# An encoder block on one core: norm rows queued behind weight splits, and TensorE kept in program order in the mixed part

## Chip, core and metric

The kernel runs on one core of one Trainium2 chip. TensorE (PE; its weight loads are PEld) multiplies into eight PSUM banks, VectorE (DVE) and ScalarE (ACT) work beside it on SBUF and PSUM, GpSimd (POOL) does a few small operations, and SyncE (SP) issues the DMAs. The metric is device time in microseconds, the median of the runs of one kernel. A line number such as L868 is a line of the kernel's file; the lines of the changed kernel stand up to eleven further down than those of the kernel before, and its new statements have numbers of their own.

## What is computed

One layer of an encoder, in float32, for 256 tokens of width 2048:

```python
mix = hybrid_mixer(x, ...)                     # grouped-query attention and latent attention
x = layer_norm(ALPHA * x + mix, ln1_g, ln1_b)
mem_n = layer_norm(mem, mem_ln_g, mem_ln_b)
xa = memory_cross_attention(x, mem_n, ...)     # 4 heads, 256 memory tokens
x = layer_norm(ALPHA * x + xa, ln2_g, ln2_b)
ff = squared_relu_mlp(x, w_mlp_in, w_mlp_out)  # jnp.square(relu(h @ w_in)) @ w_out, 8192 hidden
x = layer_norm(ALPHA * x + ff, ln3_g, ln3_b)
```

The change lies in the second layer norm's last step and in the MLP.

## The kernel before

**Products of split numbers.** Every float32 operand of a product is split into a high part (written by ACT, L87 or L936) and a low part (source minus high part, written by DVE, L88 or L937). `mm3` (L162 to L165) multiplies high by high, high by low and low by high into one PSUM bank. A 1 MB weight block `raw` arrives by one DMA and is split in pieces of 128x1024. High parts rotate through four buffers `w_hi`, low parts in the MLP through four fixed buffers `lo0` to `lo3`: a piece can be split only when the matmuls of the fourth piece before it are done.

**From cross attention to the MLP.** The matmuls L715 end the cross attention; `add_cross` adds them to `res`, `bn_stats` (L517) and two small operations give mean and deviation, L733 scales, TensorE transposes (L745), and `convert` (L750, L752, L762 or L87, L88) makes `x2t`, the MLP's transposed and split input. Ten matmuls on ones (L785) stand in a pause. All this is in program order. The residual copy `res` also needs gain and bias of the norm: `residual("ln2")` puts 16 row operations of 128x512 (L572) on the list `side`, whose entries are called one by one (`pump`) between weight splits. Those are not bound to an order, so the scheduler that builds the program places them by its own timing, and may move them ahead.

**The MLP.** The hidden layer has 4 chunks of 16 tiles of 128 columns. The first 8 tiles are computed as two groups of four (`hidden_group`, L212 and L217): group 0 with `first_pair` between its pairs of k-tiles, group 1 after it. All other tiles are mixed with the second matrix in `one_pass`, eight passes (chunk c, half q). Its list `items` alternates a hidden tile "g" (L979 and L987, 16 matmuls of 128x512 and 16 of 128x256) with a unit "u", which multiplies a pair of hidden tiles by a 1 MB block of the second matrix. Six units of each pass but the last go by a seven-product scheme (a "seven", 21 matmuls), which needs sums of the weights (`s_t`, L924) and of the hidden pair (L883); the other two take 24 matmuls. The seven products use the banks x11, x12, x21, x22 (acc) and p1, p5, p6, p7 (att). A hidden tile borrows x22, p6, p1 or p7.

**Emptying a hidden tile.** `evacuate` copies one half by ACT (L867), adds the other by DVE (L868); `finish` does relu and square (L872, L873), splits into `ht`, makes the sums and splits them into `aux`. The copy, the result and the sums are tiles `tmp`, from a ring of three.

**What sets the order.** `queue` chains the MLP's splits and weight sums on ACT and on DVE in program order, each engine by itself. The matmuls of the mixed part are not chained: the scheduler interleaves them. SP issues its DMAs in a fixed order, each when its buffer is free.

Of the kernel before, what the change touches and what calls it, by code (L numbers as in the profile page):

```python
# [38 lines left out]
def encoder_kernel(ctx: ExitStack, tc: tile.TileContext, t, out):  # L39
# [122 lines left out]
    def mm3(ps, ah, al, bh, bl, start, stop):  # L162
        nc.tensor.matmul(ps, ah, bh, start=start, stop=False)  # L163
        nc.tensor.matmul(ps, ah, bl, start=False, stop=False)  # L164
        nc.tensor.matmul(ps, al, bh, start=False, stop=stop)  # L165
# [395 lines left out]
    def residual(name):  # L561
# [284 lines left out]
    raw_x = [late.tile([P, 2048], F32, name=f"raw_x{i}") for i in range(2)]  # L846
    rings["rows"] = ctx.enter_context(tc.tile_pool(name="rows", bufs=2))
# [17 lines left out]
    def evacuate(ps, l, h, i):  # L865
        o = slice(i * S, (i + 1) * S)
        nc.scalar.activation(l[:, o], ps[:, S:2 * S], AF.Copy)  # L867
        nc.vector.tensor_tensor(out=h[:, o], in0=ps[:, 0:S], in1=l[:, o], op=ALU.add)  # L868

    def finish(h, c, p):  # L870
# [6 lines left out]
        if p in SEVEN:  # L877
            a11, a21, a12, a22 = [h[:, o:o + P] for o in range(0, 4 * P, P)]
            s = tmp_tile()
            s1, s2, s3, s4 = [s[:, o:o + P] for o in range(0, 4 * P, P)]  # L880
            for o, a, b, op in ((s1, a21, a22, ALU.subtract), (s3, a11, a21, ALU.subtract),
                                (s2, s1, a11, ALU.subtract), (s4, a12, s2, ALU.add)):
                nc.vector.tensor_tensor(out=o, in0=a, in1=b, op=op)  # L883
# [4 lines left out]
    raws, raw_of, fetched, sums = raw_x, {}, [0], deque()  # L888
    items = []
    for c, q in PASSES:  # L890
# [3 lines left out]
        for u in us:  # L894
            n = 2 if q == 0 and u[3] == CH // 2 - 2 else 1
# [3 lines left out]
    def fetch():  # L899
# [6 lines left out]
        if 1 < n < 5:  # L906
            raws.append(raw_tile())
# [21 lines left out]

    def part(src, hi=None, lo=None):  # L930
# [5 lines left out]
        queue(nc.scalar.activation(hi[:, :w], src, AF.Copy))  # L936
        queue(nc.vector.tensor_tensor(out=lo[:, :w], in0=src, in1=f(hi[:, :w]), op=ALU.subtract))  # L937
# [12 lines left out]
    def hidden_group(nexts, tiles, c, j0, beside=None):  # L950
# [20 lines left out]
    def hidden_tile(it, ps):

        _, c, j = it
        for h_ in range(2):
# [3 lines left out]
            def w_hi(k):  # L978
                nc.tensor.matmul(ps, hi[:, k * P:(k + 1) * P], x2t[:, k0 + k, :],  # L979
                                 start=k0 + k == 0, stop=k0 + k == KT - 1)  # L980
# [5 lines left out]
            for k in range(8):  # L986
                nc.tensor.matmul(ps[:, 0:S], lo[:, k * P:(k + 1) * P], x2t[:, k0 + k, 0:S],  # L987
                                 start=False, stop=False)
# [30 lines left out]
    def one_pass(c, q):  # L1019
# [28 lines left out]
        def more(ps):  # L1048
            nc.vector.tensor_tensor(out=m_t, in0=m_t, in1=ps, op=ALU.add)

        spare, n_seven, n_unit, parts = [], 0, 0, []
        while n_unit < len(order):
            it = step()
            if it[0] == "g":
                if n_unit == 0:
                    ps = x22 if it[1:] == (0, LEAD) else p6
# [10 lines left out]
            if p in sevens:  # L1067
# [218 lines left out]
```

## Time and profile before

| | us |
|---|---|
| median of 3 runs (lowest, highest) | 1121.24 (1120.96, 1121.92) |
| the profiled execution | 1121.22 |
| its span, first to last instruction | 1119.4 |
| PE busy in the span | 1084.9 |
| DVE busy | 938.6 |
| ACT busy | 637.7 |
| mean granted TensorE clock | 0.988 |

The span is 1.8 us shorter than the execution. A row of a timeline gives start, duration, engine, line, operation, output<-input, shapes, and in brackets how long the engine sat idle before it and what ended that. Matmuls overlap, so their durations are longer than the distance from one start to the next. In a row of windows, PEclk 0.50 means that TensorE was granted half its clock.

### The profile page before, as it was taken

To read this page: it belongs to the slowest core of one execution; us is meant where nothing else is said; L and a number is where in the kernel's file an instruction comes from. 1 tells how busy PE (TensorE), PEld (TensorE's weight loads), DVE (VectorE), ACT (ScalarE), POOL (GpSimd) and SP (SyncE) were. 2 spreads that over 40 slices of the span, in tenths; PEclk is the share of its full clock that TensorE was granted. 3 is DMA by queue.
4 is the path that set the end of the run, shared out by engine and by line. 5 is a ranking of instruction groups with operands and counts; after the bars stand their busy time and mean duration, and the time that the engine had idled before them with its cause. 6 is when DMAs were issued, how large, how long until landed. Compare 5 with 4: busy or idle time off the path is not lost.

```text
span 1119.4 us, 15382 instructions
## 1 busy us (share of the span) xinstructions
PE 1084.9 (97%) x5864; PEld 935.1 (84%) x5864; DVE 938.6 (84%) x1331; ACT 637.7 (57%) x925; POOL 38.2 (3%) x45
## 2 busy tenths in 40 slices
PE   8999999999999978899999999999999999999896
PEld 6988899888998867788888888888888888888685
DVE  5878677687788768879899999899999899999676
ACT  6555565546576325657467567566566566566440
POOL 1402000000100000000000000000000000000000
PEclk9999999999999989999999999999999999999898
DMA  9664454466467445445555645556646556546632
GB/s 322 239 225 151 151 188 150 152 235 241 167 223 263 151 132 177 180 143 200 206 186 206 226 166 210 196 185 221 210 169 223 189 188 225 194 182 224 227 113 76
DMA packets 37945, 215.87 MB, mean 193 GB/s; under 512 B 4336, under 2 KB 5232, under 8 KB 14192
## 3 DMA queue, kind: packets, MB, share of 16 engines
q1 hardware_dynamic: 37872, 214.89, 54.1%
q8 instruction: 46, 0.75, 0.3%
q14 instruction: 27, 0.22, 0.1%
HBM read 212.78 MB, written 2.10 MB: 192 GB/s over the span
## 4 chain that ended last, share of the span: by engine, by line
PE 94%; DVE 3%; DMA 2%; issue 1%; ACT 1%; SPq 0%; POOL 0%; DVEq 0%
PE acc L163 13%; PE acc L164 13%; PE acc L165 13%; PE acc L979 12%; PE acc L987 6%; PE att L979 6%; PE att L164 4%; PE att L163 4%; PE att L165 4%; PE att L987 3%; PE acc L205 2%; PE acc L203 2%; PE acc L204 2%; PE att L212 1%; DMA row<-in_ln_g 1%; PE acc L715 1%
## 5 line engine op out<-in xcount | busy, mean ns | idle before, releaser
L87 ACT ACTIVATE w_hi<-raw 128x1024 fp32r<-128x1024 f32 (+2 forms) x142 | 139.8, 992 | 118.2 <-PE acc L165 70.6
L88 DVE TENSOR_TENSOR w_lo<-raw,w_hi 128x1024 fp32r<-128x1024 f32 (+2 forms) x130 | 146.2, 1133 | 59.6 <-ACT w_hi L87 58.5
L937 DVE TENSOR_TENSOR lo<-raw,w_hi 128x1024 fp32r<-128x1024 f32 (+1 forms) x138 | 152.0, 1123 | 14.5 <-issue 4.9
L936 ACT ACTIVATE w_hi<-raw 128x1024 fp32r<-128x1024 f32 (+1 forms) x138 | 130.4, 975 | 34.5 <-PE acc L165 23.1
L979 PE MATMUL acc<-x2t,w_hi 128*128 128x512 f32 x576 | 149.8, 392 | 0.0
L979 PEld LDWEIGHTS acc<-x2t,w_hi 128*128 128x128 f32 x576 | 106.3, 189 | 19.3
L937 DVE TENSOR_TENSOR lo<-s_t,w_hi 128x1024 fp32r<-128x1024 f32 x84 | 102.7, 1222 | 17.5 <-ACT w_hi L936 11.9
L937 DVE TENSOR_TENSOR lo<-raw_x,w_hi 128x1024 fp32r<-128x1024 f32 x94 | 103.8, 1124 | 11.1 <-issue 4.9
L936 ACT ACTIVATE w_hi<-s_t 128x1024 fp32r<-128x1024 f32 x84 | 88.5, 1055 | 27.7 <-PE acc L165 12.0
L936 ACT ACTIVATE w_hi<-raw_x 128x1024 fp32r<-128x1024 f32 x94 | 89.2, 975 | 20.5 <-PE acc L165 10.8
L987 PEld LDWEIGHTS acc<-x2t,lo 128*128 128x128 f32 x576 | 78.6, 190 | 5.6
L979 PE MATMUL att<-x2t,w_hi 128*128 128x512 f32 x320 | 83.3, 392 | 0.0
L164 PE MATMUL acc<-lo,ht 128*128 128x512 f32 x213 | 82.2, 395 | 0.0
L987 PE MATMUL acc<-x2t,lo 128*128 128x256 f32 x576 | 80.3, 282 | 0.0
L867 ACT ACTIVATE tmp<-acc 128x256 f32<-128x256 f32 x40 | 15.2, 384 | 112.6 <-PE acc L979 111.4
L165 PE MATMUL acc<-w_hi,ht 128*128 128x512 f32 x210 | 78.8, 394 | 0.0
L163 PE MATMUL acc<-w_hi,ht 128*128 128x512 f32 x210 | 74.2, 396 | 4.6 <-ACT ht L87 4.6
L164 PE MATMUL acc<-w_lo,xt 128*128 128x512 f32 (+2 forms) x192 | 69.2, 362 | 0.0
L165 PE MATMUL acc<-w_hi,xt 128*128 128x512 f32 (+2 forms) x192 | 69.1, 361 | 0.0
L979 PEld LDWEIGHTS att<-x2t,w_hi 128*128 128x128 f32 x320 | 58.6, 189 | 10.9
L163 PE MATMUL acc<-w_hi,xt 128*128 128x512 f32 (+2 forms) x192 | 65.7, 362 | 1.8 <-ACT w_hi L87 1.8
L165 PE MATMUL acc<-w_hi,ot 128*128 128x512 f32 (+1 forms) x136 | 51.9, 382 | 0.0
(285 smaller groups left out, 2448.0 us busy)
## 6 DMA issues: line engine op xcount, KB each, us to landing
raw<-in_w_mo SPq DMA_DIRECT2D x38, 1024.0 KB, 4.8
raw<-in_w_mc SPq DMA_DIRECT2D x34, 1024.0 KB, 4.8
raw_x<-in_w_mo SPq DMA_DIRECT2D x26, 1024.0 KB, 4.8
raw_x<-in_w_mc SPq DMA_DIRECT2D x22, 1024.0 KB, 4.8
raw<-in_w_out SPq DMA_DIRECT2D x16, 1024.0 KB, 4.9
raw<-in_w_mi SPq DMA_DIRECT2D x8, 1024.0 KB, 4.9
raw<-in_w_b SPq DMA_DIRECT2D x5, 1024.0 KB, 4.8
raw<-in_w_qa SPq DMA_DIRECT2D x16, 256.0 KB, 5.4
```

The source lines that it names most:

```text
L87: pin(nc.scalar.activation(hi, src, AF.Copy), pinned)
L88: return pin(nc.vector.tensor_tensor(out=lo, in0=src, in1=f(hi), op=ALU.subtract), pinned)
L163: nc.tensor.matmul(ps, ah, bh, start=start, stop=False)
L164: nc.tensor.matmul(ps, ah, bl, start=False, stop=False)
L165: nc.tensor.matmul(ps, al, bh, start=False, stop=stop)
L203: nc.tensor.matmul(ps, hi, xt[:, k, 0:S], start=k == 0, stop=False)
L204: nc.tensor.matmul(ps, hi, xt[:, k, S:2 * S], start=False, stop=False)
L205: nc.tensor.matmul(ps, lo, xt[:, k, 0:S], start=False, stop=k == nk - 1)
L936: queue(nc.scalar.activation(hi[:, :w], src, AF.Copy))
L937: queue(nc.vector.tensor_tensor(out=lo[:, :w], in0=src, in1=f(hi[:, :w]), op=ALU.subtract))
L979: nc.tensor.matmul(ps, hi[:, k * P:(k + 1) * P], x2t[:, k0 + k, :], start=k0 + k == 0, stop=k0 + k == KT - 1)
L987: nc.tensor.matmul(ps[:, 0:S], lo[:, k * P:(k + 1) * P], x2t[:, k0 + k, 0:S], start=False, stop=False)
```

## The change

- `residual("ln2")` is replaced: after group 0, gain and bias come whole (two DMAs of 1 MB, into `s_t` and into a new buffer `row_b`), eight row operations of 128x1024 are put on `side` behind four empty entries, and they are chained by `queue`. Group 1's splits are chained too and call two entries each, so the first row operations follow the third split of group 1. A loop in `one_pass` that called what was left on `side` falls away.
- The block buffers `raw_x0`, `raw_x1` become `raw_x` and `row_b`; `row_b` serves from the fifth block on.
- `mm3` and the matmuls of `hidden_tile` go through `queue` in `one_pass`: TensorE runs them in program order.
- In the first pass two hidden tiles lead the first unit instead of one; the second of them borrows bank x21.
- `evacuate` works in place: one `tmp` tile per pair of hidden tiles instead of two. The first two hidden sums become one operation of 128x256, with two signs turned, so p7 is subtracted.

```diff
     def mm3(ps, ah, al, bh, bl, start, stop, keep=lambda ins: ins):
+        keep(nc.tensor.matmul(ps, ah, bh, start=start, stop=False))
+        keep(nc.tensor.matmul(ps, ah, bl, start=False, stop=False))
+        keep(nc.tensor.matmul(ps, al, bh, start=False, stop=stop))
...
-    raw_x = [late.tile([P, 2048], F32, name=f"raw_x{i}") for i in range(2)]
-    rings["rows"] = ctx.enter_context(tc.tile_pool(name="rows", bufs=2))
+    raw_x, row_b = [late.tile([P, 2048], F32, name=w) for w in ("raw_x", "row_b")]
...
-    def evacuate(ps, l, h, i):
+    def evacuate(ps, h, i):
         o = slice(i * S, (i + 1) * S)
-        nc.scalar.activation(l[:, o], ps[:, S:2 * S], AF.Copy)
-        nc.vector.tensor_tensor(out=h[:, o], in0=ps[:, 0:S], in1=l[:, o], op=ALU.add)
+        nc.scalar.activation(h[:, o], ps[:, S:2 * S], AF.Copy)
+        nc.vector.tensor_tensor(out=h[:, o], in0=ps[:, 0:S], in1=h[:, o], op=ALU.add)
...
-            for o, a, b, op in ((s1, a21, a22, ALU.subtract), (s3, a11, a21, ALU.subtract),
-                                (s2, s1, a11, ALU.subtract), (s4, a12, s2, ALU.add)):
-                nc.vector.tensor_tensor(out=o, in0=a, in1=b, op=op)
+            nc.vector.tensor_tensor(out=s[:, 0:2 * P].rearrange("p (i c) -> p i c", c=P),
+                                    in0=a21[:, None, :].broadcast_to([P, 2, P]),
+                                    in1=h.rearrange("p (i c) -> p i c", c=P)[:, 0:4:3, :], op=ALU.subtract)
+            nc.vector.tensor_tensor(out=s2, in0=s1, in1=a11, op=ALU.subtract)
+            nc.vector.tensor_tensor(out=s4, in0=a12, in1=s2, op=ALU.add)
...
-            n = 2 if q == 0 and u[3] == CH // 2 - 2 else 1
+            n = 2 if q == 0 and u[3] == (CH // 2 - 2 if c else 0) else 1
...
-                nc.tensor.matmul(ps, hi[:, k * P:(k + 1) * P], x2t[:, k0 + k, :],
-                                 start=k0 + k == 0, stop=k0 + k == KT - 1)
+                queue(nc.tensor.matmul(ps, hi[:, k * P:(k + 1) * P], x2t[:, k0 + k, :],
+                                       start=k0 + k == 0, stop=k0 + k == KT - 1))
...
-                    ps = x22 if it[1:] == (0, LEAD) else p6
+                    ps = {LEAD: x22, LEAD + 1: x21}[it[2]] if it[1] == 0 else p6
...
-            side.extend(residual("ln2"))
+            for w, row in (("g", s_t), ("b", row_b)):
+                nc.sync.dma_start(row, t[f"ln2_{w}"].partition_broadcast(P))
+                side.extend([lambda o=o, b=b, row=row, op=ALU.mult if w == "g" else ALU.add: queue(
+                    nc.vector.tensor_tensor(out=res[b][:, o:o + 1024], in0=res[b][:, o:o + 1024],
+                                            in1=row[:, o:o + 1024], op=op))
+                    for b in range(NB) for o in (0, 1024)])
+            side.extendleft([lambda: None] * 4)
+            s_in.split, s_in.beside = queued_split, 2
```

Three places of the order follow. **The end of the cross attention.** DVE before: the last addition to `res1` (L699), its statistics (L517, L721, L723), the first scaling (L733); the row operations are those on `row`.

```order
L699 SCALAR_TENSOR_TENSOR res1_1491<-res1_1491,acc_4109 128x256
L572 TENSOR_TENSOR res0_1490<-res0_1490,row_4444 128x512
L517 BN_STATS bn_3937<-res1_1491 128x6
L572 TENSOR_TENSOR res0_1490<-res0_1490,row_4446 128x512
L721 BN_AGGR mv_4146<-bn_3937 128x2
L723 TENSOR_SCALAR rs_v_4148<-mv_4146 128x1
L733 TENSOR_SCALAR res1_1491<-res1_1491,mv_4146,rs_r_4150 128x512
L572 TENSOR_TENSOR res1_1491<-res1_1491,row_4444 128x512
L752 TENSOR_SCALAR tmp_4157<-att_4122,gbt_112 128x256
```

DVE at the same place after the change:

```order
L700 SCALAR_TENSOR_TENSOR res1_1491<-res1_1491,acc_4109 128x256
L518 BN_STATS bn_3937<-res1_1491 128x6
L722 BN_AGGR mv_4146<-bn_3937 128x2
L724 TENSOR_SCALAR rs_v_4148<-mv_4146 128x1
L734 TENSOR_SCALAR res1_1491<-res1_1491,mv_4146,rs_r_4150 128x512
L753 TENSOR_SCALAR tmp_4157<-att_4122,gbt_112 128x256
L763 TENSOR_TENSOR x2t_4038<-tmp_4157,x2t_4038 128x256
```

No row operation stands among the statistics and the first conversions any more. There is none up to the end of group 0; four entries of twice the width follow the third and fourth split of group 1, four the fifth and sixth.

**The first unit of the mixed part.** TensorE after the change: acc_4641 is x21, which the second leading tile has just filled; att_4646 is p7 and att_4645 p6, in banks that the last two tiles of group 1 left.

```order
L984 MATMUL acc_4641<-x2t_4038,w_hi_4710 128x512
L164 MATMUL att_4643<-w_hi_4734,ht_4184 128x512
...
L164 MATMUL att_4646<-w_hi_4749,aux_4185 128x512
...
L164 MATMUL att_4645<-w_hi_4758,aux_4185 128x512
L165 MATMUL att_4645<-lo3_4189,aux_4185 128x512
L166 MATMUL att_4645<-w_hi_4758,aux_4185 128x512
L164 MATMUL acc_4641<-w_hi_4758,ht_4184 128x512
L165 MATMUL acc_4641<-lo3_4189,ht_4184 128x512
L166 MATMUL acc_4641<-w_hi_4758,ht_4184 128x512
L984 MATMUL acc_4642<-x2t_4038,w_hi_4778 128x512 x8
```

DVE after, from the last split of that unit to the operations (L868) that empty the two leading tiles out of acc_4642 and acc_4641:

```order
L934 TENSOR_TENSOR lo3_4189<-s_t_4191,w_hi_4758 128x1024
...
L934 TENSOR_TENSOR lo0_4186<-raw_4607,w_hi_4778 128x1024
L926 TENSOR_TENSOR s_t_4191<-row_b_4193 128x1024
...
L934 TENSOR_TENSOR lo1_4187<-raw_4607,w_hi_4798 128x1024
L868 TENSOR_TENSOR tmp_4624<-att_4432,tmp_4624 128x256
L868 TENSOR_TENSOR tmp_4624<-att_4433,tmp_4624 128x256
L926 TENSOR_TENSOR s_t_4191<-s_t_4191,row_b_4193 128x512 x2
...
L934 TENSOR_TENSOR lo2_4188<-row_b_4193,w_hi_4823 128x1024
L88 TENSOR_TENSOR ht_4184<-tmp_4624,ht_4184 128x2x256
L868 TENSOR_TENSOR tmp_4686<-acc_4642,tmp_4686 128x256
L868 TENSOR_TENSOR tmp_4686<-acc_4641,tmp_4686 128x256
```

DVE before, where the only leading tile is emptied out of x22 (acc_4658): between the two units' splits of block and sums.

```order
L924 TENSOR_TENSOR s_t_4191<-s_t_4191,raw_4619 128x512
L937 TENSOR_TENSOR lo0_4186<-raw_4619,w_hi_4797 128x1024
L937 TENSOR_TENSOR lo1_4187<-raw_4619,w_hi_4811 128x512
L883 TENSOR_TENSOR tmp_4648<-tmp_4639,tmp_4648 128x128
L868 TENSOR_TENSOR tmp_4706<-acc_4658,tmp_4705 128x256
L88 TENSOR_TENSOR aux_4185<-tmp_4648,aux_4185 128x512
L937 TENSOR_TENSOR lo2_4188<-s_t_4191,w_hi_4818 128x1024
L937 TENSOR_TENSOR lo3_4189<-s_t_4191,w_hi_4828 128x1024
```

The first unit's last product writes x21, and the operation that empties x21 stands on DVE behind the splits of the next hidden tile and the first split of the second unit. Before, only x22 was borrowed here, and no product of a seven writes x22.

**The end of the last pass that has hidden tiles.** TensorE before: att_4662 takes the last hidden tile, w_hi_9309 is a part of unit 6, w_hi_9329 of unit 7.

```order
L165 MATMUL acc_4657<-w_hi_9309,ht_4184 128x512
L979 MATMUL att_4662<-x2t_4038,w_hi_9249 128x512 x8
L987 MATMUL att_4662<-x2t_4038,lo2_4188 128x256 x8
L979 MATMUL att_4662<-x2t_4038,w_hi_9270 128x512 x7
L987 MATMUL att_4662<-x2t_4038,lo3_4189 128x256 x8
L979 MATMUL att_4662<-x2t_4038,w_hi_9270 128x512
L163 MATMUL acc_4656<-w_hi_9329,ht_4184 128x512
L164 MATMUL acc_4656<-lo2_4188,ht_4184 128x512
```

TensorE after: att_4646 takes the last hidden tile, w_hi_9213 and w_hi_9228 are parts of unit 6, w_hi_9248 of unit 7.

```order
L984 MATMUL att_4646<-x2t_4038,w_hi_9189 128x512 x7
L992 MATMUL att_4646<-x2t_4038,lo3_4189 128x256 x8
L984 MATMUL att_4646<-x2t_4038,w_hi_9189 128x512
L164 MATMUL acc_4640<-w_hi_9213,ht_4184 128x512
L165 MATMUL acc_4640<-lo0_4186,ht_4184 128x512
...
L166 MATMUL acc_4641<-w_hi_9228,ht_4184 128x512
L164 MATMUL acc_4640<-w_hi_9248,ht_4184 128x512
```

Unit 6 stood ahead of the last hidden tile and now stands between that tile and unit 7.

More of the change, by code (lines that the diff above doesn't have):

```diff
@@ L137, in __init__ @@
             self.ap, self.n, self.fine, self.beside, self.pinned = ap, 0, fine, beside, False
+            self.split = split
         def next(self, hi=None, lo=None):
@@ L156, in next @@
             for o in range(0, w, g):
-                split(hi[:, o:o + g], lo[:, o:o + g], self.raw[:, h * w + o:h * w + o + g],
+                self.split(hi[:, o:o + g], lo[:, o:o + g], self.raw[:, h * w + o:h * w + o + g],
                       pinned=self.pinned)
@@ L160, in next, with mm3 @@
             return hi[:, :w], lo[:, :w]
[L162 to L165, printed above, removed]
+    def mm3(ps, ah, al, bh, bl, start, stop, keep=lambda ins: ins):
+        keep(nc.tensor.matmul(ps, ah, bh, start=start, stop=False))
+        keep(nc.tensor.matmul(ps, ah, bl, start=False, stop=False))
+        keep(nc.tensor.matmul(ps, al, bh, start=False, stop=stop))
     def proj_tokens(stream, xt, nk, cols, before=None, by_block=None, wide=None, tiles=None):
@@ L566, in load @@
             for w in "gb":
-                rows[w] = rings["rows"].tile([P, 512], F32, tag="row", name="row") if "rows" in rings else tmp_tile()
+                rows[w] = tmp_tile()
                 nc.sync.dma_start(rows[w], t[f"{name}_{w}"][n * 512:(n + 1) * 512].partition_broadcast(P))
@@ L886, in finish @@
             split(y[:, 0, :], y[:, 1, :], s)
-    raws, raw_of, fetched, sums = raw_x, {}, [0], deque()
+    raws, raw_of, fetched, sums = [raw_x], {}, [0], deque()
     items = []
@@ L928, in push_sums, with queued_split @@
         add(s_t[:, 1536:2048], s_t[:, 1024:1536], b21)
+    def queued_split(hi, lo, src, pinned=False):
+        queue(nc.scalar.activation(hi, src, AF.Copy))
+        queue(nc.vector.tensor_tensor(out=lo, in0=src, in1=f(hi), op=ALU.subtract))
     def part(src, hi=None, lo=None):
@@ L986, in hidden_tile @@
             for k in range(8):
-                nc.tensor.matmul(ps[:, 0:S], lo[:, k * P:(k + 1) * P], x2t[:, k0 + k, 0:S],
-                                 start=False, stop=False)
+                queue(nc.tensor.matmul(ps[:, 0:S], lo[:, k * P:(k + 1) * P], x2t[:, k0 + k, 0:S],
+                                       start=False, stop=False))
             if h_ == 1:
@@ L991, in hidden_tile @@
         if j % 2 == 0:
-            lh[:] = [tmp_tile(), tmp_tile()]
-        evacuate(ps, *lh, j % 2)
+            now[:] = [tmp_tile()]
+        evacuate(ps, now[0], j % 2)
         if j % 2:
-            late_finish.append(lambda h=lh[1]: finish(h, c, j // 2))
+            late_finish.append(lambda h=now[0]: finish(h, c, j // 2))
     bank = []
@@ L1033, in mm @@
             left[id(ps)] -= 1
-            mm3(ps, *x, hi, lo, start, left[id(ps)] == 0)
+            mm3(ps, *x, hi, lo, start, left[id(ps)] == 0, queue)
         cols = [slice((2 * q + i) * 512, (2 * q + i + 1) * 512) for i in range(2)]
@@ L1046, in merge, with more @@
                 nc.vector.tensor_tensor(out=r, in0=r, in1=x, op=op)
-        def more(ps):
-            nc.vector.tensor_tensor(out=m_t, in0=m_t, in1=ps, op=ALU.add)
+        def more(ps, op=ALU.add):
+            nc.vector.tensor_tensor(out=m_t, in0=m_t, in1=ps, op=op)
         spare, n_seven, n_unit, parts = [], 0, 0, []
@@ L1074, in one_pass @@
                                   (raw[:, 1536:2048], ((x11, a(c, k + 1, 0)),)),
-                                  (s_t[:, 0:1024], ((p5, sm(c, p, 0)), (p7, sm(c, p, 2)))),
-                                  (s_t[:, 1024:2048], ((p6, sm(c, p, 1)), (x21, a(c, k + 1, 1))))):
+                                  (s_t[:, 0:1024], ((p5, sm(c, p, 1)), (p7, sm(c, p, 0)))),
+                                  (s_t[:, 1024:2048], ((p6, sm(c, p, 2)), (x21, a(c, k + 1, 1))))):
                     for (hi, lo), (ps, x) in zip(halves(part(src)), todo):
```

22 lines of the change are left out of this document (10 added, 12 removed).

## The prediction

> **What bounds the kernel now.** I read the page's busy shares first, then TensorE's waits, then windows over the places where it waited, then timelines there.
>
> ```profile
> span 1119.4 us, 15382 instructions
> PE 1084.9 (97%) x5864; PEld 935.1 (84%) x5864; DVE 938.6 (84%) x1331; ACT 637.7 (57%) x925; POOL 38.2 (3%) x45
> PE att L745 <- DVE res L733: 5.5, 2, 4.4
> PE acc L163 <- ACT ht L87: 4.6, 1, 4.6
> PE att L164 <- DVE lo L937: 3.4, 1, 3.4
> PE acc L212 <- DVE x2t L88: 2.9, 2, 1.8
> PE acc L212 <- ACT x2t L750: 2.3, 1, 2.3
> PE att L987 <- DVE lo L937: 1.4, 3, 0.5
> PE att L163 <- ACT w_hi L936: 1.0, 2, 0.8
> ```
>
> TensorE bounds it: no matmul is removed, so only its waits and its slow stretches can be won. These waits sum to 21.1 us and all lie in or behind the turn from cross attention to the MLP. Windows of 3.41 us over three places show a second price (columns: length, busy time of PE, PEld, DVE, ACT, POOL, granted clock, DMA):
>
> ```profile
> 396.56:399.98 3.42, 0.44 (x4) 0.14 (x1) 1.93 (x5) 0.00 (x0) 0.00 (x0) 1.00 0.33 83
> 399.98:403.39 3.41, 1.12 (x4) 0.72 (x4) 1.54 (x4) 0.56 (x1) 0.54 (x1) 0.50 0.00 0
> 406.80:410.21 3.41, 3.41 (x14) 3.02 (x13) 2.22 (x5) 0.25 (x1) 0.00 (x0) 0.50 0.14 32
> 423.87:427.28 3.41, 1.64 (x12) 1.32 (x11) 2.65 (x6) 2.03 (x3) 0.00 (x0) 1.00 0.85 233
> 471.66:475.07 3.41, 0.06 (x1) 0.00 (x0) 3.41 (x8) 0.30 (x2) 0.00 (x0) 1.00 0.69 238
> 475.07:478.48 3.41, 3.36 (x8) 2.69 (x9) 1.91 (x4) 1.83 (x3) 0.00 (x0) 0.50 0.67 216
> 1051.92:1055.34 3.42, 0.62 (x5) 0.30 (x3) 2.92 (x4) 1.52 (x3) 0.00 (x0) 1.00 0.19 26
> 1058.75:1062.16 3.41, 3.41 (x10) 2.65 (x9) 0.00 (x0) 0.00 (x0) 0.00 (x0) 0.50 0.49 204
> ```
>
> A window with 0.62 us of work or less is followed by half clock, one with 1.64 us is not; full clock returns after a full window. So a wait of some 3 us costs, besides itself, half of the work done until the clock is back.
>
> **Step 1, the early rows go.** Behind the wait of 4.4 us:
>
> ```profile
> 397.94 0.69 DVE L572 TENSOR_TENSOR res<-res,row 128x512 f32<-128x512 f32 x1 [2.46 <-DMA row<-in_ln_g]
> 398.55 0.42 DVE L517 BATCH_NORM_STATS2 bn<-res 128x6 f32<-128x256 f32 x1
> 400.78 0.55 DVE L733 TENSOR_SCALAR res<-res,mv,rs_r 128x512 f32<-128x512 f32 x1 [0.66 <-POOL rs_r L726]
> 401.39 1.12 PE L745 MATMUL att<-ident,res 128*128 128x128 f32 x4 [4.38 <-DVE res L733]
> 404.77 2.05 PE L212 MATMUL acc<-x2t,wide 128*128 128x512 f32 x4 [2.26 <-ACT x2t L750]
> 410.48 1.17 PE L212 MATMUL acc<-x2t,wide 128*128 128x512 f32 x4
> 410.48:434.16 23.68, 19.57 (x115) 16.55 (x114) 18.95 (x28) 12.04 (x18) 0.00 (x0) 1.00 0.53 181
> 434.16 1.09 PE L212 MATMUL att<-x2t,w_hi 128*128 128x512 f32 x4
> 459.42 1.98 PE L979 MATMUL acc<-x2t,w_hi 128*128 128x512 f32 x8
> ```
>
> The last statistics stand behind a row operation that waits 2.46 us for its DMA and takes 0.61 us to the next start; a second one (0.6) follows. Without them L733 starts 3.67 us earlier, at 397.1, and the transposes at 397.7. From there to the first matmul (404.77) it takes 3.38 us, with two more row operations (1.2) in the conversions: without them, 2.2, so the first matmul starts at 399.9 (-4.9). Up to 410.48 two k-tiles and transposes ran at half clock in 5.71 us; at full clock a pair with its transposes takes 19.57 / 6 = 3.3. So the row of 410.48 comes at 403.2: **-7.3**. The next six pairs took 23.68 us with 19.57 busy; the 4.1 us of waits were for DVE, which had ten row operations among 18.95 us of work. Without them 12.5 us of DVE work stand beside 19.6 on TensorE, and ACT has 12.0: **-4.1**. Bounds: -3.7 (only the statistics earlier) to -11.4.
>
> The clock there: the window of 396.56 held 0.44 us; now it gets four transposes more (some 0.6), so 1.0, between the 0.62 that cost the clock and the 1.64 that did not. If lost, 3.41 us run at half: 1.7. I take half: **+0.9**. The Trainium skill ("TensorE: Matmul & The Clock Gate", Part 4) says that transposes do not count as busy for the clock; by that rule the loss is sure and the time is 0.8 longer. No window here tells: in that of 423.87 transposes are only a part.
>
> **Step 2, the start of the mixed part.** Before, the second unit waits 0.77 and 3.40 us for splits and 3.41 us then run at half clock (row 475.07): 0.8 + 3.4 + 1.7 = 5.9, which falls away as such: **-5.9**. What is late instead follows from the order of DVE, counted from the start of group 1 (434.16 before).
>
> ```profile
> 441.41 1.09 PE L212 MATMUL acc<-x2t,w_hi 128*128 128x512 f32 x4
> 442.54 1.06 ACT L87 ACTIVATE w_hi<-raw 128x1024 fp32r<-128x1024 f32 x1
> 1034.97 3.49 DVE L937 TENSOR_TENSOR lo<-raw,w_hi 128x1024 fp32r<-128x1024 f32 x3
> L924 DVE TENSOR_TENSOR s_t<-raw 128x1024 f32<-128x1024 f32 x25 | 30.5, 1220 | 0.0
> 442.87 0.75 DVE L868 TENSOR_TENSOR tmp<-acc,tmp 128x256 f32<-128x256 f32 x2
> 444.98 1.02 DVE L883 TENSOR_TENSOR tmp<-tmp 128x128 f32<-128x128 f32 x4
> 464.99 0.40 PE L163 MATMUL att<-w_hi,ht 128*128 128x512 f32 x1
> 1044.09 1.07 PE L163 MATMUL acc<-w_hi,ht 128*128 128x512 f32 x4
> ```
>
> Group 1's fourth split needs the buffers that group 0's last pair of k-tiles reads until 442.5 (row 441.41); its high part starts 8.4 us after group 1 and is there at 9.5. The two row operations ahead of it follow the third split, whose buffers come free with group 1's start: 1.1 on ACT, 1.1 on DVE, 2.3 for the rows, so DVE idles from 4.5 on, and from 9.5 on nothing holds it. Until the L868 that empties x21 the order lists 23 operations of 1024 columns (15 splits, 6 rows, 2 weight sums), 12 of 512, 14 of 256, 8 of 128. Distances between starts: (3.49 - 1.22) / 2 = 1.135 for 1024, 0.61 for 512 (397.94 to 398.55), 0.36 for 256 (0.75 for two), 0.25 for 128 (1.02 for four): 26.1 + 7.3 + 5.0 + 2.0 = 40.4, so x21 is free at 49.9. The row operation of 1024 is not in the trace; it lies between 1.135 (an addition with the same operands' size, L924, is as long as a split) and 2 x 0.61. I take 1.135. The sum of 256 columns lies between 0.36 and two of 0.25.
>
> TensorE reaches that product after group 1 (459.42 - 434.16 = 25.3), two hidden tiles (464.99 - 459.42 = 5.5 each, 11.0) and six products (18 matmuls at (1.07 - 0.39) / 3 = 0.227, 4.1): 40.4. Two splits of group 1 behind the rows come about 0.5 late (the sixth ends at 9.5 + 7 x 1.135 + 0.75 = 18.2; with a ninth of 25.3 per piece, the last pair of group 0 being one, it is wanted at 6 x 2.8 and four matmuls, 17.7): **+1.1**, so 41.5. The wait is 49.9 - 41.5 = **+8.4**, of which p7 and p6, emptied in the same stretch, may take a first part. Behind it the next pieces are split, so the second unit does not wait. A wait of 8.4 us leaves an almost empty window; the clock stays half for 3.4 to 6.8 us of work after it, on average 5.1: **+2.5**. Together +12.0. Bounds: 0 if the bank were free in time, +17 if DVE also stalls on ACT by 10% of its 40 us.
>
> **Step 3, program order at the end of the hidden tiles.**
>
> ```profile
> 1052.15 0.39 PE L979 MATMUL att<-x2t,w_hi 128*128 128x512 f32 x1
> 1057.15 0.80 PE L163 MATMUL acc<-w_hi,ht 128*128 128x512 f32 x1 [4.61 <-ACT ht L87]
> ```
>
> Unit 7 needs the hidden tile that ended with row 1052.15; emptying, relu, square and splitting took 5.0 us, with TensorE idle for 4.61. The clock was half until 1062.16, 5.0 us of work: 2.5. Now unit 6 stands there with 24 x 0.227 = 5.4 us, which hides the 5.0: **-7.1**. Were the chain longer by one split (1.2), 0.8 would come back.
>
> The three waits of 0.46 at the turn from first to second half of a chunk lose their cause, but the last hidden tile then takes p7 as soon as DVE has read it: **-0.7**, between 0 and -1.4.
>
> **At nothing.** Evacuation in place has the same two operations per half. The eight DMAs of 256 KB become two of 1 MB, the same bytes, wanted 20 us later. One buffer less leads the blocks, but the first unit's block, behind the third-last release, is wanted only after two hidden tiles. In the steady part program order costs nothing as long as the low parts come in time (rival below).
>
> **The sum.** -7.3 - 4.1 + 0.9 - 5.9 + 1.1 + 8.4 + 2.5 - 7.1 - 0.7 = -12.2. The profiled execution took 1121.2 us with a span of 1119.4, as the median: **1109 us**, own range 1104 to 1114.
>
> **Rivals.**
>
> *The conversions set the pace, not the rows* (0.13): ACT and DVE take turns per pair, and only the 3.7 us of the statistics are won. 1109 + 7.7 = 1117. Against it: DVE's 12.5 of 19.6 us.
>
> *x21 is free in time* (0.13), because DVE is not held at 9.5: then 10.9 of step 2 falls away, 1098. Against it: the buffers' reader of row 441.41 stands in the same place of the order.
>
> *Program order makes each seven wait* (0.07): in the trace the matmuls of high parts run ahead while low parts are late. The latest is that of the last sums:
>
> ```profile
> 1031.43 0.40 PE L979 MATMUL acc<-x2t,w_hi 128*128 128x512 f32 x1
> 1033.22 1.23 DVE L937 TENSOR_TENSOR lo<-s_t,w_hi 128x1024 fp32r<-128x1024 f32 x1 [0.24 <-ACT w_hi L936]
> ```
>
> It is there at 1034.45; in program order it is wanted 16 matmuls after the hidden tile, at 1031.66 + 3.63 = 1035.29, a margin of 0.84. Were DVE 1.34 us later in every one of the 42 sevens, each would lose 0.5, 21 us: 1130, slower. It decides from 12.2 / 42 = 0.29 us per seven.
>
> That the rows still run early is excluded by the order.
>
> **The numbers.** Forecast 0.67, rivals 0.13, 0.13, 0.07. The range 1101 to 1117 holds the forecast's cases and most of the first rival, leaving out the third, most of the second and the far tail. What counts as a difference is 0.2%, about what a measurement of this kernel can tell: faster 0.89, same 0.04, slower 0.07.
>
> **What would show it.** Step 1: no row operation before group 1, group 1 starting near 423. Step 2: a wait of about 8 us in the first unit, for DVE's L868, and half clock behind it; without it the second step is wrong. Step 3: no wait in the last pass at unit 7. A wait per seven would show the third rival.

## The result and the profile after

The changed kernel takes **1111.53 us** (median of 6 runs, 1108.15 to 1112.74) where the kernel before takes 1121.31 beside it (6 runs, 1120.96 to 1122.33): ratio 0.9908, 95% interval 0.9894 to 0.9921. The page of the changed kernel's profiled execution, and its list of TensorE's waits (total us, times, longest):

```profile
span 1109.8 us, 15290 instructions
...
PE 1082.2 (98%) x5864; PEld 934.4 (84%) x5864; DVE 937.4 (84%) x1299; ACT 640.3 (58%) x925; POOL 38.3 (3%) x45
...
PE att L164 <- DVE tmp L868: 5.3, 1, 5.3
PE att L984 <- DVE m_t L1054: 3.3, 3, 1.1
PE acc L164 <- DVE tmp L868: 2.4, 1, 2.4
PE acc L213 <- ACT x2t L751: 1.6, 1, 1.6
PE acc L166 <- DVE ht L88: 1.4, 1, 1.4
...
```

The waits of 4.4, 4.6 and 3.4 us of before are gone. New are 5.3 and 2.4 us for emptied banks (L868), one of 1.4 for `ht` (L88) and three of 1.1 for `m_t` (L1054).

To place the difference, each kernel's lost time was counted through its trace: for every matmul the distance to the next start, less the median distance for its shape (227 ns for 512 columns, 120 for 256), summed from 390 us on (up to there both kernels do the same work), and read off in both where the same amount of product work was done. Half clock counts as lost.

| stretch (end of it before / after) | lost before | lost after | difference | prediction |
|---|---|---|---|---|
| step 1: to the pairs ahead of group 1 (432.7 / 420.7) | 15.3 | 3.0 | **-12.3** | -10.5 |
| step 2: to the third unit (488.0 / 481.1) | 7.3 | 12.4 | **+5.1** | +6.1 |
| seven passes with the four turns (1042.0 / 1038.3) | 4.0 | 7.2 | **+3.2** | -0.7 |
| step 3: the rest | 7.2 | 0.6 | **-6.6** | -7.1 |
| sum | 33.8 | 23.2 | **-10.6** | -12.2 |

The span fell by 9.6. Of the 1.0 that is missing, 0.4 lie behind the last matmul, and 0.6 ahead of 390 us, where nothing was changed. Rows of TensorE's timeline (matmuls on ones, transposes, the first product, the start of group 1, three products of the first unit):

```profile
395.05 2.32 PE L786 MATMUL att<-ones 128*128 128x512 bf16 x10
...
398.30 0.66 PE L746 MATMUL att<-ident,res 128*128 128x128 f32 x4 [0.71 <-DVE res L734]
400.52 1.17 PE L213 MATMUL acc<-x2t,wide 128*128 128x512 f32 x4 [1.57 <-ACT x2t L751]
...
422.44 1.09 PE L213 MATMUL att<-x2t,w_hi 128*128 128x512 f32 x4
...
458.86 0.40 PE L164 MATMUL att<-w_hi,ht 128*128 128x512 f32 x1
...
467.06 0.77 PE L164 MATMUL att<-w_hi,aux 128*128 128x512 f32 x1 [5.30 <-DVE tmp L868]
...
472.35 0.80 PE L164 MATMUL acc<-w_hi,ht 128*128 128x512 f32 x1 [2.39 <-DVE tmp L868]
```

The same kernel's VectorE rows that end the two waits, and the windows there (length, busy PE, PEld, DVE, ACT, POOL, clock, DMA):

```profile
466.50 0.74 DVE L868 TENSOR_TENSOR tmp<-att,tmp 128x256 f32<-128x256 f32 x2
...
471.55 0.75 DVE L868 TENSOR_TENSOR tmp<-acc,tmp 128x256 f32<-128x256 f32 x2
```

```profile
422.44:458.86 36.42, 36.42 (x211) 31.90 (x210) 33.09 (x44) 20.10 (x28) 0.00 (x0) 1.00 0.66 245
...
460.70:464.12 3.42, 1.06 (x5) 0.56 (x3) 3.42 (x5) 3.41 (x6) 0.00 (x0) 1.00 0.01 2
464.12:467.53 3.41, 0.47 (x1) 0.50 (x2) 3.41 (x6) 0.25 (x1) 0.00 (x0) 0.50 0.00 0
467.53:470.94 3.41, 2.43 (x6) 1.32 (x5) 3.15 (x6) 3.23 (x7) 0.00 (x0) 0.50 0.89 308
470.94:474.36 3.42, 2.01 (x5) 1.62 (x6) 2.63 (x8) 2.38 (x5) 0.00 (x0) 0.50 0.00 0
474.36:477.77 3.41, 3.41 (x11) 2.73 (x10) 2.15 (x5) 1.39 (x3) 0.00 (x0) 0.50 0.28 53
```

Group 1 and two hidden tiles run without a gap (36.42 of 36.42). Then the first unit waits for p7 and for x21, 7.7 us together, and the clock stays at half for four windows, 13.65 us, of which 8.3 are busy, 4.2 more than at full clock. VectorE is busy nearly throughout.

### The profile page after: what moved, and what is told of

It reads as the page before. It is cut to its first block, busy times and chain, and to the rows that moved or that the text cites. A ratio compares the mean times of both kernels' runs of the same rounds, so it can differ in the third digit from the quotient of the medians.

```text
span 1109.8 us, 15290 instructions
## 1 busy us (share of the span) xinstructions
PE 1082.2 (98%) x5864; PEld 934.4 (84%) x5864; DVE 937.4 (84%) x1299; ACT 640.3 (58%) x925; POOL 38.3 (3%) x45
## 4 chain that ended last, share of the span: by engine, by line
PE 91%; DVE 5%; DMA 2%; ACT 1%; issue 0%; SPq 0%; POOL 0%; DVEq 0%; ACTq 0%
PE acc L164 12%; PE acc L166 12%; PE acc L165 12%; PE acc L984 12%; PE acc L992 6%; PE att L984 5%; PE att L164 4%; PE att L166 4%; PE att L165 4%; PE att L992 3%; PE acc L206 2%; PE acc L204 2%; PE acc L205 2%; DVE lo L934 2%; PE acc L213 1%; PE att L213 1%
## 5 line engine op out<-in xcount | busy, mean ns | idle before, releaser
L87 ACT ACTIVATE w_hi<-raw 128x1024 fp32r<-128x1024 f32 (+2 forms) x134 | 131.6, 989 | 115.5 <-PE acc L166 70.9
L88 DVE TENSOR_TENSOR w_lo<-raw,w_hi 128x1024 fp32r<-128x1024 f32 (+2 forms) x130 | 146.1, 1132 | 60.1 <-ACT w_hi L87 58.8
L934 DVE TENSOR_TENSOR lo<-raw,w_hi 128x1024 fp32r<-128x1024 f32 (+1 forms) x146 | 161.7, 1123 | 8.0 <-ACT w_hi L933 4.7
L933 ACT ACTIVATE w_hi<-raw 128x1024 fp32r<-128x1024 f32 (+1 forms) x146 | 139.9, 979 | 43.2 <-PE acc L166 24.8
L984 PE MATMUL acc<-x2t,w_hi 128*128 128x512 f32 x592 | 155.0, 394 | 0.0
L984 PEld LDWEIGHTS acc<-x2t,w_hi 128*128 128x128 f32 x592 | 110.0, 190 | 20.1
L164 PE MATMUL acc<-w_hi,ht 128*128 128x512 f32 x210 | 82.4, 392 | 2.6 <-DVE tmp L868 2.4
L166 PE MATMUL acc<-w_hi,ht 128*128 128x512 f32 x210 | 82.1, 391 | 1.4 <-DVE ht L88 1.4
L984 PE MATMUL att<-x2t,w_hi 128*128 128x512 f32 x304 | 79.1, 392 | 3.3 <-DVE m_t L1054 3.3
L934 DVE TENSOR_TENSOR lo<-raw_x,w_hi 128x1024 fp32r<-128x1024 f32 (+1 forms) x48 | 53.5, 1129 | 3.9 <-ACT w_hi L933 3.7
L164 PE MATMUL att<-w_hi,aux 128*128 128x512 f32 x131 | 51.6, 394 | 5.3 <-DVE tmp L868 5.3
L934 DVE TENSOR_TENSOR lo<-row_b,w_hi 128x1024 fp32r<-128x1024 f32 (+1 forms) x46 | 51.1, 1125 | 2.3 <-ACT w_hi L933 2.2
```

The lines of the kernel that those rows point to most:

```text
L87: pin(nc.scalar.activation(hi, src, AF.Copy), pinned)
L88: return pin(nc.vector.tensor_tensor(out=lo, in0=src, in1=f(hi), op=ALU.subtract), pinned)
L164: keep(nc.tensor.matmul(ps, ah, bh, start=start, stop=False))
L166: keep(nc.tensor.matmul(ps, al, bh, start=False, stop=stop))
L933: queue(nc.scalar.activation(hi, src, AF.Copy))
L934: queue(nc.vector.tensor_tensor(out=lo, in0=src, in1=f(hi), op=ALU.subtract))
```

## The experiments

Each ratio is against the kernel before on the same chip.

### The rows alone

The kernel before with only the eight row operations queued behind group 1's third split, the buffers that they need (`s_t`, `row_b`) and group 1's chained splits; no other part of the change.

```diff
-            side.extend(residual("ln2"))
+            for w, row in (("g", s_t), ("b", row_b)):
+                nc.sync.dma_start(row, t[f"ln2_{w}"].partition_broadcast(P))
...
+            side.extendleft([lambda: None] * 4)
+            s_in.split, s_in.beside = queued_split, 2
```

> The kernel before with one part of the change alone: the eight row operations queued behind group 1's third split, with s_t and the second raw buffer as the rows' buffers; one leading tile, two buffers per pair, the scheduler's order on TensorE, four operations per hidden sum. Theory: group 1 starts 12 us earlier (at 422.5 instead of 434.2 us), as in the changed kernel; VectorE's backlog then meets a first unit with one tile's cover less and pairs that take two of the three buffers, so that this stretch loses 10 to 16 us where the kernel before loses 7.3; the wait of 4.61 us with 2.5 of half clock at the last pass stays: 1121.3 - 12 + 3 to 9 = 1112 to 1118 us, likeliest 1115. Rival (the rows are worth their 12 us by themselves, and the other parts only mend the rest): 1109 us or less. Rival 2 (the rows alone only move the loss): 1119 us or more.

Measured: 1115.28 us, ratio 0.9943 (0.9929 to 0.9957). Its waits:

```profile
PE att L164 <- DVE tmp L868: 7.3, 2, 5.9
PE acc L164 <- ACT ht L87: 4.6, 1, 4.6
```

Up to the start of group 1 it has the whole gain, as much as the changed kernel (counted as above, 12.3 us less lost than before at that point). Of these 12.3, 6.8 are left behind the second unit: the banks' emptying is waited for 7.3 us, and 6.8 us run at half clock. The wait of 4.6 at the last pass stays. So the gain of step 1 is the rows' alone, and the price of step 2 is theirs as well: it is there without the second leading tile.

### TensorE in free order

The changed kernel without `queue` around the matmuls of the mixed part.

```diff
...
-            mm3(ps, *x, hi, lo, start, left[id(ps)] == 0, queue)
+            mm3(ps, *x, hi, lo, start, left[id(ps)] == 0)
...
```

> The changed kernel with TensorE's matmuls of the mixed part left to the scheduler's order again; everything else of the change stays. Theory (program order brings step 3): at the end of pass (3,0) the eighth unit waits again for the last hidden tile's emptying, relu, square and split, some 4.6 us with half clock behind it (2.5), so +7.1; the three waits of 1.11 us at the turns from first to second half of a chunk, which the changed kernel has and the kernel before had at 0.46, shrink by some 0.65 each, -2.0: 1111.5 + 5 = 1116.5 us (1114 to 1119). Rival (the hidden tiles' cover comes from the two tiles that lead, not from the order): no wait at the eighth unit, 1109.5 to 1111.5 us. Second rival (program order costs every seven something): faster than 1109 us.

Measured: 1114.88 us, ratio 0.9934 (0.9922 to 0.9947). The row of its eighth unit in the last pass but one, and the windows there:

```profile
1049.00 0.80 PE L164 MATMUL acc<-w_hi,ht 128*128 128x512 f32 x1 [4.61 <-ACT ht L87]
```

```profile
1043.43:1046.85 3.42, 0.96 (x8) 0.64 (x6) 2.58 (x3) 1.33 (x2) 0.00 (x0) 1.00 0.28 38
1046.85:1050.26 3.41, 1.26 (x3) 1.07 (x4) 1.93 (x3) 1.89 (x3) 0.00 (x0) 0.50 0.84 334
1050.26:1053.68 3.42, 3.42 (x9) 2.65 (x9) 0.00 (x0) 0.00 (x0) 0.00 (x0) 0.50 0.58 242
```

The wait and its half clock are back exactly; lost time against the changed kernel rises there by 7.1 us. Elsewhere the free order is in part better: 4.2 us less are lost at the first unit, where the next hidden tile's matmuls stand ahead of the product that waits for x21, and 4.3 less at the four turns together, where no wait for `m_t` is left. In the steady stretches between the turns, however, it loses 0.4 to 1.5 us each against program order, 4.1 in all. So program order costs nothing per seven (the third rival is out); it gains 7 at one place and pays some of it back at those where something is late.

### One leading tile

```diff
-            n = 2 if q == 0 and u[3] == (CH // 2 - 2 if c else 0) else 1
+            n = 2 if q == 0 and u[3] == CH // 2 - 2 else 1
...
-                    ps = {LEAD: x22, LEAD + 1: x21}[it[2]] if it[1] == 0 else p6
+                    ps = x22 if it[1:] == (0, LEAD) else p6
```

> The changed kernel with one hidden tile instead of two ahead of the first unit (the bank x21 then holds no tile when the first unit wants it, and the second double tile comes ahead of unit 6, as in the other chunks). Theory A (DVE is behind with its whole queue at the start of the mixed part, and whichever bank it empties late is waited for): p7, still holding a tile of group 1, is waited for some 3 us longer (the wait of 5.3 becomes about 8, since 5.5 us of TensorE's cover and 2.6 us of DVE's work go), the wait of 2.4 for x21 goes, the half clock behind it stays within 1 us: 1111.5 us, 1109.5 to 1113. Theory B (the bank x21, held by the second leading tile, is the cause, as the prediction's step 2 named it): the waits and the half clock of 11.9 us fall away, 1100 to 1104 us.

Measured: 1109.19 us, ratio 0.9882 (0.9866 to 0.9899). Its two long waits on TensorE's timeline:

```profile
456.40 0.76 PE L164 MATMUL att<-w_hi,ht 128*128 128x512 f32 x1 [3.03 <-DVE tmp L868]
...
466.45 3.64 PE L984 MATMUL acc<-x2t,w_hi 128*128 128x512 f32 x8 [3.55 <-DVE tmp L868]
```

Theory B is out: without a tile in x21 TensorE still waits 6.6 us for L868, now for p1 (a tile of group 1) and then for x22. But the place was expected wrongly: p1, not p7. The second leading tile is not what the changed kernel gains by: without it the ratio is 0.9882 against 0.9908, the intervals just touch.

### Where the emptying stands: buffers, rows, and place

Three runs on what holds L868. First a fourth buffer in the ring of `tmp`:

```diff
-    rings["tmp"] = ctx.enter_context(tc.tile_pool(name="tmp_late", bufs=3))
+    rings["tmp"] = ctx.enter_context(tc.tile_pool(name="tmp_late", bufs=4))
```

> The changed kernel with four buffers instead of three in the ring of tiles that hidden pairs are emptied into; TensorE's order is the same. Theory (the emptying of group 1's last pair waits for one of these buffers, not for DVE alone): L868 for p7 then stands some 5 us earlier in DVE's queue, at about 460 us, so the wait of 5.3 us goes; x21 is emptied some 5 us earlier, at about 467.5, and waited for 4.4 us; half clock behind it 3.4 instead of 4.1: 1111.5 - 3.3 - 0.7 = 1107.5 us, 1105.5 to 1109.5. Rival (only the sum of DVE's work counts): the first wait goes and the second grows by as much, 1110.5 to 1112 us.

Measured: 1107.91 us, ratio 0.9875 (0.9861 to 0.9888). Then four rows instead of two behind the third split, in VectorE's gap:

```diff
+            pairs = [[side.popleft(), side.popleft()] for _ in range(2)]
+            side.extendleft([lambda r=r: [x() for x in r] for r in reversed(pairs)])
             side.extendleft([lambda: None] * 4)
```

> The changed kernel with four row operations instead of two behind the third split of group 1, four behind the fourth as two and two with the next (the same eight in all). In the changed kernel's trace VectorE is idle for 2.98 us ahead of the fourth split, which two more rows (2.3 us) fill. Theory (VectorE's backlog sets the waits of 5.3 and 2.4 us in the first unit): everything behind comes 2.3 us earlier, the two waits together are 5.4 us, half clock behind them 0 to 1.7 us less: 1108.5 us, 1107 to 1110. Rival (the emptying of p7 waits for its buffer, and that for ScalarE, not for VectorE's sum): the waits stay at 7.7 us, 1111 to 1112 us.

Measured: 1106.44 us, 0.6 under the range that was expected, ratio 0.9867 (0.9853 to 0.9880). And both together, with the edit of the turn below:

> The changed kernel with three edits together: four buffers in the ring of hidden pairs, four rows behind the third split, the last hidden tile of a turn in p6. Theory (each takes a loss of its own): from the run with four buffers, 1107.9, the three waits of the turns go (-3.3), and the wait of 5.0 us for x21 shrinks by the 2.3 us of the rows (-2.3, with half clock 0 to 1.7 more): 1102 us, 1100.5 to 1103.5. Rival (the rows and the buffers mend the same wait, so that the second brings nothing): 1104 to 1105 us.

Measured: 1105.80 us, ratio 0.9858 (0.9844 to 0.9871). The line of the wait in each of the three (four buffers; early rows; together):

```profile
PE acc L164 <- DVE tmp L868: 5.0, 1, 5.0
```

```profile
PE acc L164 <- DVE tmp L868: 4.8, 1, 4.8
```

```profile
PE acc L164 <- DVE tmp L868: 4.8, 1, 4.8
```

Each edit takes the wait of 5.3 us for p7 away, and what is left, for x21, is the same 4.8 to 5.0 in all three. It was 2.4 in the changed kernel: with four buffers x21 comes free 5 us earlier, but TensorE, no longer held at p7, wants it 7.6 us earlier (462.36 for 469.96). The rival of the third run holds, at 0.8 us above its range: the two edits mend the same wait. VectorE's queue in the combined run shows why the rest does not shrink:

```profile
460.32 1.23 DVE L934 TENSOR_TENSOR lo<-raw,w_hi 128x1024 fp32r<-128x1024 f32 x1 [0.15 <-ACT w_hi L933]
461.47 1.22 DVE L926 TENSOR_TENSOR s_t<-row_b 128x1024 f32<-128x1024 f32 x1
...
463.20 1.22 DVE L934 TENSOR_TENSOR lo<-raw,w_hi 128x1024 fp32r<-128x1024 f32 x1
...
464.67 0.68 DVE L926 TENSOR_TENSOR s_t<-s_t,row_b 128x512 f32<-128x512 f32 x1
...
465.88 0.74 DVE L868 TENSOR_TENSOR tmp<-acc,tmp 128x256 f32<-128x256 f32 x2
```

Ahead of the L868 that TensorE waits for stand splits of the next hidden tile and weight sums of the next unit, 4.0 us of work (1.14 + 1.14 + 1.14 + 0.60) that TensorE needs only behind the product that waits: they are chained by `queue`, the emptying is not, and the scheduler put it behind them. The next run, with the four buffers and the early rows but without the edit of the turn, writes the emptying of the two leading tiles ahead of the first unit's last two products, and chains it:

```diff
+        if c == 0 and j in (LEAD, LEAD + 1):
+            lead_out.append(lambda h=now[0]: evacuate(ps, h, j % 2, queue))
+        else:
...
+                    if todo[0][0] is p6:
+                        while lead_out:
+                            lead_out.pop(0)()
```

> The run with four buffers and four early rows (without the tile in p6, which brought nothing), and in it the emptying of the two leading tiles written ahead of the first unit's last two products and kept in that place of the queues of ScalarE and VectorE; in both combined runs so far these stood behind the splits and sums of the next tile and unit, and x21 was waited for 4.8 us although VectorE's backlog was smaller. Theory (not the amount of VectorE's work, but the place of this L868 in its queue is what the wait of 4.8 us is): x21 is emptied at about 462.5 us instead of 466.6, the wait is about 1 us, and no half clock follows it (1.7): 1105.8 - 3.8 - 1.7 = 1100.3 us, 1099 to 1102.5. Rival (the amount: what is put off waits one unit later): a wait of 3 to 5 us in the second unit for its splits or its sums, 1104 to 1106 us.

Measured: 1101.69 us, ratio 0.9825 (0.9811 to 0.9838). Its row of the wait, and VectorE's rows:

```profile
463.86 0.50 PE L164 MATMUL acc<-w_hi,ht 128*128 128x512 f32 x1 [1.04 <-DVE tmp L868]
```

```profile
463.06 0.75 DVE L868 TENSOR_TENSOR tmp<-acc,tmp 128x256 f32<-128x256 f32 x2
...
464.86 1.22 DVE L926 TENSOR_TENSOR s_t<-row_b 128x1024 f32<-128x1024 f32 x1
```

The wait is 1.04 us, no window there falls to half clock, and the second unit waits 0.3 us once. So 3.8 of the 4.8 us were the place in the queue, not the amount of work.

### The turns

```diff
-                    spare = spare or [p1, p7]
+                    spare = spare or [p1, p6]
```

> The changed kernel with the second hidden tile behind the sevens put into p6 instead of p7; TensorE's order is the same. Theory (the three waits of 1.11 us at the turns of the chunks 1 to 3 are for VectorE's reading of p7, the last of the three steps m_t+p6, merge, m_t-p7, which lies some 5 us behind that of p6): the three waits go, 1111.5 - 3.3 = 1108.2 us, 1107 to 1109.5. Rival (VectorE is late there as such, and the tile then waits for its low parts instead): waits for L934 of some 0.5 to 1.1 each in their place, 1110 to 1111.5 us.

Measured: 1110.68 us, ratio 0.9905 (0.9892 to 0.9919), no difference that can be told from the changed kernel. In the changed kernel the last turn reads so on TensorE and VectorE:

```profile
1037.84 2.09 PE L984 MATMUL att<-x2t,w_hi 128*128 128x512 f32 x8 [1.11 <-DVE m_t L1054]
```

```profile
1033.54 0.69 DVE L1051 TENSOR_TENSOR res<-res,m_t 128x512 f32<-128x512 f32 x1
...
1035.87 1.22 DVE L934 TENSOR_TENSOR lo<-raw_x,w_hi 128x1024 fp32r<-128x1024 f32 x1
1037.01 0.68 DVE L1054 TENSOR_TENSOR m_t<-m_t,att 128x512 f32<-128x512 f32 x1
```

With the tile in p6, the waits for `m_t` are gone, and the list has in their place:

```profile
PE acc L166 <- DVE ht L88: 3.4, 3, 1.4
```

The tile ends earlier, and the eighth unit then waits 1.01 us twice for the split of its hidden pair (the wait of 1.4 is the first turn's, as in the changed kernel). Two of the three waits have only moved; that of the last turn is gone. The last run adds to the two edits so far (leading tiles out in place, p6) that one merge instead of two follows each split:

```diff
         if banks:
             pump()
         if sums:
             sums.popleft()()
-        else:
-            pump()
```

> As the run with the leading tiles emptied in place, and besides the last hidden tile of a turn in p6, and one merge of the sevens' sums behind each split instead of two where no sum is due. Theory (at the turns the split of the last hidden pair, L88, waits behind merges that VectorE could do later; with p6 alone the wait of 1.11 us only went over to it, 0.99 us each): one or two merges of 0.6 us less stand ahead of it, the waits of 1.42, 0.99 and 0.99 us shrink to 0.3 or less, about 2.5 us less than the other run of this pair with its three waits of 1.11 and one of 1.42 (4.7 in all, of which 0.3 to 1.5 stay): 3.2 to 4.4 us less than it. Rival (VectorE's sum of work at the turn counts): no more than 0.5 us less than it.

Measured: **1099.51 us** (1099.05 to 1100.22), ratio 0.9804 (0.9791 to 0.9818), the best version, 1.1% below the changed kernel by the medians. It is 2.2 us less than the run without the edits of the turn, between theory and rival: the three waits for `m_t` are gone, three for `ht` stay:

```profile
PE acc L166 <- DVE ht L88: 3.0, 3, 1.0
```

Most of this is the tile in p6, which alone had brought these waits from 4.7 to 3.4 us. With one merge fewer behind each split only the first turn's wait shrinks, from 1.42 to 0.98; the other two stay at 1.00. What holds these was not separated.

### The rows on GpSimd

```diff
-                    nc.vector.tensor_tensor(out=res[b][:, o:o + 1024], in0=res[b][:, o:o + 1024],
+                    nc.gpsimd.tensor_tensor(out=res[b][:, o:o + 1024], in0=res[b][:, o:o + 1024],
```

> The changed kernel with the eight row operations of 128 x 1024 on GpSimd instead of VectorE (9.1 us of DVE's work less ahead of the first unit). Theory (DVE's backlog is what the first unit waits for): both waits, 7.7 us, and the half clock of 4.1 behind them go, 1099.5 us, 1098 to 1102.5. Rival (GpSimd is slower than DVE's 1.14 us for such an operation, and slows DVE's operations beside it, as the Trainium skill (GPSIMD Engine, shared SBUF port) has it): DVE's splits of group 1 become longer than 1.135 us from start to start, or the loads into the rows' buffers come late and TensorE waits for them: 1106 us or more.

Measured: 1104.73 us, ratio 0.9852 (0.9839 to 0.9866), between the two. Its waits show both: none for L868, but 2.4 us in group 1:

```profile
PE att L218 <- DVE lo L934: 2.4, 1, 2.4
```

Groups of VectorE's instructions from 424 to 441 us, of GpSimd's from 416 to 440 (busy, mean ns):

```profile
L934 DVE TENSOR_TENSOR lo<-raw,w_hi 128x1024 fp32r<-128x1024 f32 x5 | 14.2, 2881 | 0.0
...
L753 DVE TENSOR_SCALAR tmp<-att,gbt 128x256 f32<-128x256 f32 x1 | 0.5, 530 | 0.0
```

```profile
L1149 POOL TENSOR_TENSOR res<-res,row_b 128x1024 f32<-128x1024 f32 x4 | 12.8, 3246 | 0.0
```

While GpSimd does its rows, a split takes VectorE 2.88 us. Against the changed kernel 6.1 us more are lost up to the end of group 1, half clock behind that wait included, and 12.0 are won back at the first unit.

## Why the prediction was right, point by point

The sign, the size (1109 forecast, 1111.5 measured, inside its own range of 1104 to 1114) and the three steps held, the second in part by luck; one small term had the wrong sign.

**Step 1 held.** Transposes at 398.30 for 397.7, first product at 400.52 for 399.9, group 1 at 422.44 for "near 423", and no row operation ahead of it; the run with the rows alone has the same gain. The difference of 1.8 (-12.3 for -10.5) is by half the clock term: +0.9 was added as half a chance, and this execution did not lose it. The chance was mis-sized. Of the eleven profiles with this front (the changed kernel and ten runs) one had it, that with the tile in p6:

```profile
393.49:396.91 3.42, 3.42 (x22) 2.12 (x21) 2.82 (x8) 0.00 (x0) 0.39 (x1) 1.00 0.00 0
396.91:400.32 3.41, 1.13 (x7) 0.80 (x7) 1.88 (x4) 1.52 (x3) 0.16 (x1) 1.00 0.00 0
400.32:403.73 3.41, 3.41 (x12) 2.82 (x11) 2.92 (x7) 0.63 (x2) 0.00 (x0) 0.50 0.02 5
```

There a window happened to begin just behind the ten matmuls on ones, and its 1.13 us of work, 0.74 of them transposes, cost the clock. In the changed kernel's own execution the window boundaries (464.12 less twenty times 3.413) fall at 395.86 and 399.27, so that 1.5 us of those matmuls count in, and the clock stays. The prediction carried the boundaries of before over as if they were fixed. By the rule of the Trainium skill that it weighed ("TensorE: Matmul & The Clock Gate", Part 4, transposes do not count) the loss was to be sure; ten of eleven profiles do not show it. Part 1 of the same page of the Trainium skill says that the window runs freely, so that the point of transition depends on where in it the work lands; that the traces bear out. Against the first of these two rules the transposes count here, as two of the runs show together: with GpSimd's rows 1.46 us of products alone were followed by half clock, and with one leading tile 1.76 us, of which 0.66 are transposes, were not:

```profile
425.56:428.98 3.42, 1.46 (x8) 1.33 (x9) 3.42 (x2) 0.65 (x1) 3.42 (x2) 1.00 0.77 295
428.98:432.39 3.41, 3.41 (x13) 2.95 (x13) 3.41 (x2) 1.06 (x1) 3.41 (x2) 0.50 0.10 14
```

```profile
398.12:401.53 3.41, 1.76 (x9) 1.38 (x10) 2.04 (x6) 1.58 (x3) 0.00 (x0) 1.00 0.00 0
401.53:404.95 3.42, 3.42 (x24) 3.07 (x23) 2.79 (x6) 1.18 (x3) 0.00 (x0) 1.00 0.00 0
```

Its 1.10 us of products alone would have been too little. By these windows the 1.0 us of the forecast would have lost the clock at the boundaries of before, transposes counted or not; what kept it is where the boundaries fell.

**Step 2 held, in part by luck.** x21 was forecast free 49.9 us after group 1's start; 471.55 + 0.75 - 422.44 = 49.86. That this agrees to the tenth is luck, for two errors cancel. The forecast let VectorE stand idle until 9.5 us, for the matmuls that read the high parts. In the changed kernel its fourth split of group 1 waits for those that read the low parts (L218) and starts at 7.5 us; from there the same operations take 42.35 us, not 40.4, since VectorE is idle for 1.75 of them, 1.14 in one wait for ScalarE:

```profile
429.95 1.23 DVE L934 TENSOR_TENSOR lo<-raw,w_hi 128x1024 fp32r<-128x1024 f32 x1 [2.98 <-PE acc L218]
...
460.15 1.23 DVE L934 TENSOR_TENSOR lo<-s_t,w_hi 128x1024 fp32r<-128x1024 f32 x1 [1.14 <-ACT w_hi L933]
```

But for the wait for p7 the product would want x21 after 40.7 (forecast 40.4 and 1.1 for late splits, which did not come: 36.42 of 36.42 us are work). p7 takes the larger part of the wait, as was allowed for; together 7.7 for 8.4, with 4.2 of half clock for 2.5, since the second wait kept a window from filling. What the prediction did not see is the reason: it counted the queue ahead of L868 as work that has to be done first, and the run with the emptying in place shows that 4 us of it do not. The prediction's word for the cause, the bank that the second leading tile borrows, is too narrow: with one leading tile p1 and x22 are waited for instead.

**Step 3 held.** No wait at the eighth unit; -6.6 for -7.1, and the run in free order brings 4.61 and 6.83 us of half clock back.

**The turns were wrong.** "The three waits of 0.46 [...] lose their cause, but the last hidden tile then takes p7 as soon as DVE has read it: -0.7, between 0 and -1.4." The stretch loses 3.2 us more instead. In program order TensorE reaches p7 before VectorE's third step on `m_t`, which stands behind four splits and a merge, and has nothing to put in between: 1.11 us at three turns; in free order none of these waits is there. The first turn waits 1.42 for a split of `ht` instead. The bound of zero was set without asking where in VectorE's queue that reading stands, which step 2 had asked for its own bank. This 3.9 is the largest error of the sum; steps 1 and 2 gave 2.8 of it back, step 3 and what lies outside the table took 1.5, and the span's fall is 2.6 short of the forecast.

**The rivals.** Conversions do not set the pace of the pairs (from 400.52 to the first unit TensorE does not wait); x21 is not free in time, though VectorE is held only until 7.5; no seven waits.

## What to carry to other kernels

When one engine is late, read its queue ahead of the instruction that is waited for, and ask of each entry who needs it next: here moving two short operations ahead of 4 us of early work was worth 4 us, where less work ahead or a further buffer took the first wait and left 4.8 to 5.0 us at the next bank. Program order on the engine that sets the time is worth most where the next independent piece can stand over a latency, and it turns every late bank into a wait; so ask at each place what it would have done meanwhile. A wait mended at one bank can go on to the next operation of the same late queue, as at two of the turns.

## What the runs showed of the hardware

- Beside GpSimd's row operations (two inputs of 128x1024, 3.1 to 3.2 us each) VectorE's subtractions of the same size took 2.88 us instead of 1.22, about one for each operation of GpSimd, while its operation with one input tile from PSUM (L753) kept its 0.53. The Trainium skill ("SBUF — State Buffer", Who interferes with whom) has it that the two share a pair of ports as an exclusive lock, taken by an operation of VectorE with two inputs in SBUF and not by one with one input at most; the trace agrees in both.
- The windows of 3.41 us by which the clock is granted lie differently in each execution (boundaries at 399.98 before, at 399.27 after, at 400.32 with the tile in p6), and a wait of about 5 us was followed by one such window at half clock with four buffers (3.41 us), by two with early rows (6.83), by four in the changed kernel, where a second wait followed (13.65).
- A window with up to 1.46 us of work was followed by half clock (run with GpSimd's rows), one with 1.57 us was not (free order, 459.75 to 463.17), where the traces of before had bounded that between 0.62 and 1.64. Transposes on the identity count as work: 1.76 us with them kept the clock, 1.10 of it products.
